# Where the convolution of a finished tile pair is issued inside the next Strassen unit

## The chip, the cores and the metric

The kernel runs on one core of a Trainium2 chip. The metric is device time in microseconds (us) of one execution, the median of several runs. TensorE multiplies, ScalarE runs activations and copies, VectorE (DVE in the rows) does the additions, GpSimd (POOL) issues the accumulating DMAs, and SyncE (SP) issues the plain loads.

## The reference, cut to what matters

One decoder layer on 512 tokens of width 2048. The part that the change touches is the first half of the gated MLP: an up-projection, a causal convolution of width 3 along the tokens, and a product of the two halves.

```python
def conv_ffn(h, w_up, conv_w, conv_b, w_down):
    u = h @ w_up                                   # (512, 2048) @ (2048, 2 * 5632)
    up = jnp.pad(u, ((0, 0), (CONV_WIDTH - 1, 0), (0, 0)))
    u = conv_b + sum(conv_w[i] * up[:, i:i + S] for i in range(CONV_WIDTH))
    a, b = jnp.split(u, 2, axis=-1)
    return (jax.nn.silu(a) * b) @ w_down
```

Everything is float32. A matmul operand is split into two parts, a rounded one and the rest, and products of parts are summed.

## The kernel before

**Units.** The up-projection makes 44 pairs of output tiles (128 channels by 512 tokens; tile `a` of the pair goes through the SiLU, tile `b` does not). Three pairs come from plain matmuls. The other 41 come from `unit`, one call for each pair (L228): a Winograd-Strassen product of 2x2 blocks, in which seven products named B11, T1, T2, B21, T3, B22 and T4 are issued in this order. Each is 8 matmuls of 512 columns with the rounded weights and 8 of 256 columns with the rest (T1: 16 of 256 and 8 of 256). A unit has three PSUM banks: r1 takes B11 and B21, r3 takes T1 and B22, and r2 takes T2, T3 and T4, each after the additions that read what was there before. For T3 these are L279 and L281, for T4 they are L294 and L296. Units alternate between the bank groups `acc` and `att`, so a unit's T4 and the next unit's B11 stand side by side in TensorE's queue.

**Weights.** A unit loads five 512 KB tiles, a11, a21, a22, a12 and d, into eight buffers named `raw` (L135, issued by SP). GpSimd adds a second block to d by an accumulating DMA (L242, `raw<-in_w_up`). L271 adds a22 to a21 (the sum s, for T1), L275 adds a11 to s (T2), and L299 adds s to a12 (B22). `parts` makes the two operands of each product: a rounded copy on ScalarE (L140, `wh`, three buffers) and the rest on VectorE (L142, `wl`, three buffers). Seven pairs of these are needed for a unit.

**Order.** The order of the instructions on each engine is fixed when the kernel is built, by a planner that takes what it reckons to be ready, earlier lines of the program first. Each engine then works through its own list. `issue_after` (in `behind`) adds that an instruction is queued behind a named one on its engine. In the profiled lists L271 of the next unit stands ahead of L275 of the unit at hand.

**The work between.** A unit calls `between(0)` after the copy of T1's bank, `between(1)` after the copies of B21's bank (L285, L287). In the up-projection the convolution of the pair before is issued at `between(1)`, all of it in a steady unit: `finish` with two `conv` (one activation L1032 and two additions of scaled shifts, L1033 and L1034, for each tile), the SiLU L1039, the product L1041 and the DMA of the result L1042.

Of the kernel before, what the change touches and what calls it, by code (L numbers as in the profile page):

```python
# [15 lines left out]
ALU = mybir.AluOpType  # L16
# [14 lines left out]
HALF = S // 2  # L31
# [44 lines left out]
def block_kernel(ctx: ExitStack, tc: tile.TileContext, A: dict, out: bass.AP):  # L76
# [11 lines left out]
    def t2k(tag, bufs, dt=F32, w=S):  # L88
        return sb.tile([P, w], dt, tag=tag, bufs=bufs, name=nm(tag))
# [7 lines left out]
    def slot(dt=F32, group=""):  # L97

        o = spare.pop((dt, group), None)
        if o is None:  # L100
            t = two(dt)
            o, spare[dt, group] = t[:, :S], t[:, S:]
        return o
# [12 lines left out]
    tt = nc.vector.tensor_tensor  # L116
# [16 lines left out]
    def load(src, w=1024):  # L133
        raw = t2k("raw", 8, w=w)
        nc.sync.dma_start(raw, src)  # L135
        return raw

    def parts(raw, w=1024):
        wh = t2k("wh", 3, F32R, w)
        act(wh, raw, AF.Copy)  # L140
        wl = t2k("wl", 3, F32R, w)
        tt(wl, raw, wh.bitcast(F32), ALU.subtract)  # L142
        return wh, wl
# [63 lines left out]
    def both(t):  # L207
        return t[:, :HALF], t[:, HALF:]
# [19 lines left out]
    def unit(src, f, between=lambda *_: None, wide=False, by_dma=False):  # L228

        n = len(f)
        w = n * P
        bank = (acc, att)[units[0] % 2]
        units[0] += 1
        r1, r2, r3 = (bank() for _ in range(3))

        def add(o, more):
            nc.gpsimd.dma_start(o, more, accum_op=ALU.add)  # L242

        def product(ps, a, name, first):
            ah, al = a
            for p in range(n):
                ops = [f[p][name]] if wide and name != "T1" else both(f[p][name])
                for i, b in enumerate(ops):
                    mm(ps[:, : b.shape[1]], ah[:, p * P : (p + 1) * P], b, start=first and p + i == 0, stop=False,  # L249
                       skip_group_check=True)  # L250
            for p in range(n):
                mm(ps[:, :HALF], al[:, p * P : (p + 1) * P], f[p][name][:, :HALF], start=False, stop=p == n - 1,  # L252
                   skip_group_check=True)

        a11 = load(src[0], w)
        a21 = load(src[2], w)
        a22 = load(src[3], w)
        a12 = load(src[1], w)
        if by_dma:
            d = load(src[2], w)  # L260
            add(d, src[0])
        product(r1, parts(a11, w), "B11", True)
        p = t2k("ta", 2)
        p1, p5 = both(p)
        if wide:
            act(p1, r1[:, HALF:], AF.Copy)
            last_v = tt(p1, r1[:, :HALF], p1, ALU.add)
        else:
            act(p1, r1[:, :HALF], AF.Copy)
        s = a21 if by_dma else t2k("raw", 8, w=w)  # L270
        last_v = tt(s, a21, a22, ALU.add)  # L271
        product(r3, parts(s, w), "T1", True)
        last = act(p5, r3[:, :HALF], AF.Copy, scale=-1.0)
        between(0, last, last_v)
        tt(s, s, a11, ALU.add)  # L275
        product(r2, parts(s, w), "T2", True)
        e = t2k("sp", 2)
        l1, u2 = both(e)
        last_v = tt(u2, p1, r2[:, :HALF], ALU.subtract)  # L279
        if wide:  # L280
            last_v = tt(u2, u2, r2[:, HALF:], ALU.subtract)  # L281
        product(r1, parts(a12, w), "B21", False)
        spare.pop((F32, "c"), None)
        c1, c2 = slot(group="c"), slot(group="c")
        last = act(c1[:, :HALF], r1[:, :HALF], AF.Copy)  # L285
        if wide:
            last = act(l1, r1[:, HALF:], AF.Copy)  # L287
        between(1, last, last_v)
        if by_dma:
            product(r2, parts(d, w), "T3", False)  # L290
        else:
            tt(a11, a11, a21, ALU.add)
            product(r2, parts(a11, w), "T3", False)
        tt(c2[:, HALF:], r2[:, :HALF], p1, ALU.subtract)  # L294
        if wide:
            tt(c2[:, HALF:], r2[:, HALF:], c2[:, HALF:], ALU.add)  # L296
        else:
            tt(c2[:, HALF:], c2[:, HALF:], p5, ALU.add)
        tt(a12, a12, s, ALU.add)  # L299
        product(r3, parts(a12, w), "B22", False)  # L300
        if wide:
            act(c1[:, HALF:], r3[:, :HALF], AF.Copy)
            tt(u2, r3[:, HALF:], u2, ALU.add)
            add(c1, e)
        else:
            tt(c1[:, HALF:], r3[:, :HALF], u2, ALU.add)
        product(r2, parts(a22, w), "T4", False)
        if wide:
            act(c2[:, :HALF], r2[:, :HALF], AF.Copy)
            tt(p1, r2[:, HALF:], p1, ALU.subtract)  # L310
            add(c2, p)
        else:
            tt(c2[:, :HALF], r2[:, :HALF], p1, ALU.subtract)
        return c1, c2
# [20 lines left out]
    @contextmanager  # L335
    def behind(*pins):

        with ExitStack() as stack:
            for p in pins:
                stack.enter_context(tc.issue_after(p.ins))  # L340
            yield
# [139 lines left out]
    for c in range(2):  # L481
        w = prep(A["w_qi7"][c])
        for k in range(8):
            i = 8 * c + k
# [153 lines left out]
    def some_ada(n=1, tag=("raw", 8)):  # L638
        for _ in range(n):
            if ada_left:  # L640
                ada_half(cb, *ada_left.pop(0), tag)
# [11 lines left out]
    for u in range(32):  # L653

        def between(i, *pins):
            with behind(*pins):
                next(work)
                if i:
                    some_ada()

        pair = unit(A["w_x"][u], f, between)
        for i, o in enumerate(pair):
            if u >= 16:
                sig = act(o, o, AF.Sigmoid)
            save(xd[2 * u + i], o)
# [138 lines left out]
    def stick_2(zs, soft):  # L804

        for n in (1, 2, 0):
            sp = of_soft(soft)[n]
            last = stt(sp, zs[n][:, : sp.shape[1]], 0.0, sp, ALU.max, ALU.add)
        one, two, three, _ = strips(*of_soft(soft))
        later = t2k("T", 2)  # L810
        a, b = later[:, 2 * P : 3 * P], later[:, : 2 * P]
        tt(a, two[:, P:], one, ALU.add)
        tt(b[:, :P], three[:, P : 2 * P], two[:, :P], ALU.add)
        tt(b[:, P:], three[:, 2 * P :], a, ALU.add)
        return (a, b), last
# [39 lines left out]
    for hd in range(NH):  # L855
# [12 lines left out]
        later, last = stick_2(*state)  # L868
# [32 lines left out]
    def sparse_2(p, s):  # L901
        nc.vector.reciprocal(s, s)
        for b in (2, 0, 1, 3):
            last = ts(p[b], p[b], s[:, b : b + 1], None, ALU.mult)
        return last
# [39 lines left out]
    for hd in range(NH):  # L945
        p, s, last = sparse_1(*pairs[hd])
# [7 lines left out]
        last = sparse_2(p, s)  # L954
# [14 lines left out]
    for j in range(KT):  # L969
# [9 lines left out]
        last = tt(g, g, t, ALU.add)  # L979
# [18 lines left out]

    def between(i, *pins):
        with behind(*pins):  # L1000
            if i:
                some_ada()

    sums = []
    for u in range(KT // 2):
        xr = []
        for j in (2 * u, 2 * u + 1):
            xr.append(t2k("w", 2))
            nc.gpsimd.dma_start(xr[-1], A["x"][j])
        for i, c in enumerate(unit(A["w_o"][u], f, between)):  # L1010
            j = 2 * u + i
            stt(c, c, mod[:, 32 + j : 33 + j], xr[i], ALU.mult, ALU.add)
            nc.gpsimd.dma_start(x1d[j], c)
            squares(c, j, sums)
# [15 lines left out]
    def conv(u, j):  # L1030
        t = t2k(("w", "T")[j % 2], 2)
        act(t, u, AF.Identity, scale=cw[:, j, 2:3], bias=cw[:, j, 3:4])  # L1032
        stt(t[:, 1:], u[:, : S - 1], cw[:, j, 1:2], t[:, 1:], ALU.mult, ALU.add)  # L1033
        stt(t[:, 2:], u[:, : S - 2], cw[:, j, 0:1], t[:, 2:], ALU.mult, ALU.add)  # L1034
        return t

    def finish(j, ua, ub):
        a = conv(ua, 2 * j)
        act(a, a, AF.Silu)  # L1039
        b = conv(ub, 2 * j + 1)  # L1040
        tt(a, a, b, ALU.mult)  # L1041
        nc.gpsimd.dma_start(yd[j // 2][:, j % 2 * S : (j % 2 + 1) * S], a)  # L1042


    ups = [bank() for bank in (acc, att) for _ in range(NU)]
# [27 lines left out]
    ups = [evac(ps) for ps in ups]  # L1073
    ready = [(j, *ups[2 * j : 2 * j + 2]) for j in range(NU)]

    def between(i, *pins):
        if len(ready) > 1 - i:
            with behind(*pins):
                finish(*ready.pop(0))

    finish(*ready.pop(0))
    for j in range(NU, NJ):
# [60 lines left out]
    def add_first(j, o):  # L1143
        t = t2k("w", 2)
        save(t, sumd[j])
        tt(o, o, t, ALU.add)
        save(sumd2[j], o)

    def between(i, *pins):
        if ready:  # L1150
            with behind(*pins):
                add_first(*ready.pop(0))

# [35 lines left out]
    j = KT - 1  # L1189
    ps = acc(), acc()  # L1190
    prepare(j)
    last = t2k("w", 2)
# [111 lines left out]
```

## Time and profile before

| what | value |
|---|---|
| median of 3 runs | 2863.05 us (2857.27 to 2873.1) |
| the profiled execution, its own time | 2858.4 us |
| its span on the core | 2856.6 us |
| granted clock of TensorE, mean of the span | 0.995 |
| the stage of the 41 units (first L296 to last L296) | 828.7 us for 40 units |

The span runs from the first to the last instruction of the program; the time of the execution holds it and 1.8 us around it. Busy times are sums over the records of an engine. An engine's idle time is put down to what released the next instruction.

### The profile page before, as it was taken

Reading aid. Unit: us, or ns where it says so; the run is one execution under the profiler, and the core shown is the slowest. Engines: PE = TensorE matmul, PEld = TensorE weight load, DVE = VectorE, ACT = ScalarE, POOL = GpSimd, SP = SyncE. Lnnn points to the kernel's source line nnn. Section 1 sums busy time; section 2 is a strip of 40 time slices with the busy share of each in tenths; the row PEclk is TensorE's granted clock in tenths of the full one; section 3 lists DMA queues with packets and bytes.
Section 4 is the critical chain, followed back from the end, with each engine's and each line's share of the span. In section 5 each row is a group of like instructions: output and inputs, shape, how many; then the busy total and the mean of one; then the engine's idle time right before and its main releaser. Section 6 shows DMA issues by size and latency. Waiting matters only on the chain.

```text
span 2856.6 us, 44877 instructions
## 1 busy us (share of the span) xinstructions
PE 2772.5 (97%) x17174; PEld 2464.7 (86%) x17174; DVE 2370.6 (83%) x3489; ACT 1410.4 (49%) x2083; POOL 391.6 (14%) x588
## 2 busy tenths in 40 slices
PE   7999999999999999999989999999999999999998
PEld 6779999999998768889988888888888888887887
DVE  8979888888897898899988888788888887887555
ACT  5544444455546655444465545455555555444221
POOL 0000000001011202111301111111111111111111
PEclk9999999999999999999999999999999999999999
DMA  9964456655565548665446767777677777668654
GB/s 348 347 228 143 166 179 211 201 177 171 180 225 191 180 152 303 242 197 203 155 159 165 200 178 193 184 190 196 182 199 184 200 192 239 176 196 292 230 185 137
DMA packets 176167, 576.88 MB, mean 202 GB/s; under 512 B 22144, under 2 KB 26624, under 8 KB 175952
## 3 DMA queue, kind: packets, MB, share of 16 engines
q1 hardware_dynamic: 123312, 421.06, 43.5%
q0 software_dynamic: 52192, 152.57, 20.3%
q8 instruction: 135, 2.21, 0.3%
q14 instruction: 80, 0.66, 0.1%
q10 hardware_dynamic: 448, 0.39, 0.0%
HBM read 487.78 MB, written 60.46 MB: 192 GB/s over the span
## 4 chain that ended last, share of the span: by engine, by line
PE 58%; DVE 16%; DMA 12%; issue 8%; ACT 5%; POOL 0%; DVEq 0%; SPq 0%; ACTq 0%; POOLq 0%
PE acc L249 12%; PE att L249 12%; DMA raw<-in_w_up 9%; DVE wl L142 6%; PE acc L252 6%; PE att L252 6%; ACT wh L140 3%; PE acc L152 3%; PE acc L153 3%; PE acc L154 3%; PE att L154 3%; PE att L152 3%; PE att L153 3%; DVE raw L333 2%; DVE raw L275 2%
## 5 line engine op out<-in xcount | busy, mean ns | idle before, releaser
L140 ACT ACTIVATE wh<-raw 128x1024 fp32r<-128x1024 f32 (+2 forms) x787 | 809.7, 1041 | 945.0 <-DVE raw L275 197.9
L142 DVE TENSOR_TENSOR wl<-raw,wh 128x1024 fp32r<-128x1024 f32 (+2 forms) x787 | 940.4, 1209 | 149.9 <-ACT wh L140 148.7
L249 PE MATMUL acc<-F,wh 128*128 128x256 f32 (+1 forms) x3840 | 653.6, 318 | 11.8 <-DVE F L296 7.1
L249 PE MATMUL att<-F,wh 128*128 128x256 f32 (+1 forms) x3776 | 640.2, 318 | 16.0 <-DVE F L296 9.0
L249 PEld LDWEIGHTS acc<-F,wh 128*128 128x128 f32 x3840 | 544.4, 191 | 60.9 <-DVE F L296 12.5
L249 PEld LDWEIGHTS att<-F,wh 128*128 128x128 f32 x3776 | 533.4, 191 | 65.8 <-DVE F L296 14.7
L252 PE MATMUL acc<-F,wl 128*128 128x256 f32 x2520 | 352.3, 283 | 0.0
L252 PE MATMUL att<-F,wl 128*128 128x256 f32 x2464 | 344.5, 282 | 0.0
L252 PEld LDWEIGHTS acc<-F,wl 128*128 128x128 f32 x2520 | 333.8, 191 | 11.9
L252 PEld LDWEIGHTS att<-F,wl 128*128 128x128 f32 x2464 | 326.3, 191 | 11.4
L333 DVE SCALAR_TENSOR_TENSOR raw<-raw,raw 128x1024 f32<-128x1024 f32 x186 | 226.9, 1230 | 70.4 <-DMA raw<-in_w_ada 70.4
L152 PE MATMUL acc<-F,wh 128*128 128x512 f32 (+2 forms) x476 | 179.0, 385 | 15.7 <-ACT F L173 15.7
L153 PE MATMUL acc<-F,wh 128*128 128x512 f32 (+2 forms) x476 | 182.2, 383 | 0.0
L154 PE MATMUL acc<-F,wl 128*128 128x512 f32 (+2 forms) x476 | 181.8, 382 | 0.0
L271 DVE TENSOR_TENSOR raw<-raw,raw 128x1024 f32<-128x1024 f32 x89 | 108.8, 1222 | 79.8 <-DMA raw<-in_w_up 70.8
L154 PE MATMUL att<-F,wl 128*128 128x512 f32 x394 | 155.5, 395 | 6.1 <-DVE wl L142 6.1
L152 PE MATMUL att<-F,wh 128*128 128x512 f32 x394 | 154.0, 397 | 2.7 <-ACT wh L140 2.7
L153 PE MATMUL att<-F,wh 128*128 128x512 f32 x394 | 154.8, 393 | 0.3 <-DVE F L174 0.2
L152 PEld LDWEIGHTS acc<-F,wh 128*128 128x128 f32 (+1 forms) x476 | 88.9, 188 | 35.4 <-ACT F L173 17.5
L275 DVE TENSOR_TENSOR raw<-raw,raw 128x1024 f32<-128x1024 f32 x89 | 109.5, 1230 | 1.0
L299 DVE TENSOR_TENSOR raw<-raw,raw 128x1024 f32<-128x1024 f32 x89 | 108.8, 1222 | 1.4
L153 PEld LDWEIGHTS acc<-F,wh 128*128 128x128 f32 (+1 forms) x476 | 89.4, 188 | 19.2 <-DVE F L174 1.8
(307 smaller groups left out, 3427.0 us busy)
## 6 DMA issues: line engine op xcount, KB each, us to landing
raw<-in_w_up SPq DMA_DIRECT2D x205, 512.0 KB, 4.4
raw<-in_w_ada SPq DMA_DIRECT2D x186, 512.0 KB, 5.0
raw<-in_w_x SPq DMA_DIRECT2D x128, 512.0 KB, 4.0
raw<-in_w_down SPq DMA_DIRECT2D x64, 512.0 KB, 4.5
raw<-in_w_up POOLq DMA_DIRECT2D x41, 512.0 KB, 8.8
xd<-F POOLq DMA_DIRECT2D x64, 256.0 KB, 2.6
F<-xd POOLq DMA_DIRECT2D x64, 256.0 KB, 5.0
raw<-in_w_o SPq DMA_DIRECT2D x32, 512.0 KB, 3.9
```

Source lines behind the costliest of these rows:

```text
L140: act(wh, raw, AF.Copy)
L142: tt(wl, raw, wh.bitcast(F32), ALU.subtract)
L152: mm(ps, ah, bh, start=first, stop=False, skip_group_check=not check)
L153: mm(ps, ah, bl, start=False, stop=False, skip_group_check=not check)
L154: mm(ps, al, bh, start=False, stop=last, skip_group_check=not check)
L249: mm(ps[:, : b.shape[1]], ah[:, p * P : (p + 1) * P], b, start=first and p + i == 0, stop=False, skip_group_check=True)
L252: mm(ps[:, :HALF], al[:, p * P : (p + 1) * P], f[p][name][:, :HALF], start=False, stop=p == n - 1, skip_group_check=True)
L271: last_v = tt(s, a21, a22, ALU.add)
L275: tt(s, s, a11, ALU.add)
L299: tt(a12, a12, s, ALU.add)
L333: stt(raw, raw, 1.0, cb[half], ALU.mult, ALU.mult, accum_out=macc[:, t, half : half + 1])
```

## The change

`finish` is cut into three steps, and `unit` calls `between` in a third place, after L296 and the addition that reads r2 last before T4. In a steady unit of the up-projection the convolution of tile `a` with its SiLU is now issued at `between(0)`, the convolution of tile `b` at `between(1)`, and the product of the two with the DMA of the result at `between(2)`, pinned behind the addition of L296 on VectorE. The other stages ignore the third place. The first of the 41 units, which has two pairs to finish, does one whole at `between(0)` and the second in steps.

```diff
@@ unit
         if wide:
-            tt(c2[:, HALF:], r2[:, HALF:], c2[:, HALF:], ALU.add)
+            last_v = tt(c2[:, HALF:], r2[:, HALF:], c2[:, HALF:], ALU.add)
         else:
-            tt(c2[:, HALF:], c2[:, HALF:], p5, ALU.add)
+            last_v = tt(c2[:, HALF:], c2[:, HALF:], p5, ALU.add)
+        between(2, last, last_v)
         tt(a12, a12, s, ALU.add)
@@
-    def finish(j, ua, ub):
+    def finish_steps(j, ua, ub):
         a = conv(ua, 2 * j)
         act(a, a, AF.Silu)
+        yield
         b = conv(ub, 2 * j + 1)
+        yield
         tt(a, a, b, ALU.mult)
         nc.gpsimd.dma_start(yd[j // 2][:, j % 2 * S : (j % 2 + 1) * S], a)
+        yield
+
+    def finish(*args):
+        for _ in finish_steps(*args):
+            pass
@@
+    steps = []
+
     def between(i, *pins):
-        if len(ready) > 1 - i:
-            with behind(*pins):
+
+        with behind(*pins):
+            if i == 0 and len(ready) > 1:
                 finish(*ready.pop(0))
+                return
+            if not steps:
+                steps.append(finish_steps(*ready.pop(0)))
+                if i == 1:
+                    next(steps[0])
+            next(steps[0])
+            if i == 2:
+                steps.pop()
```

The input-projection's `between` returns at once for i == 2, the one of the output projection acts for i == 1 alone, and the one of the down-projection for i < 2.

## Rows read from the trace of the kernel before

**Rows 1.** The page, part 1: busy us of each engine.

```profile
PE 2772.5 (97%) x17174; PEld 2464.7 (86%) x17174; DVE 2370.6 (83%) x3489; ACT 1410.4 (49%) x2083; POOL 391.6 (14%) x588
```

**Rows 2.** Busy time by windows: 40 units, then one late unit.

```profile
1535.32:2364.02 828.70, 806.39 (x4808) 707.73 (x4807) 693.26 (x883) 429.18 (x645) 126.80 (x159) 1.00 0.72 192
...
2283.78:2303.43 19.65, 19.65 (x123) 17.62 (x122) 17.50 (x23) 10.88 (x17) 3.21 (x4) 1.00 0.74 200
```

**Rows 3.** Waits of TensorE in the 40 units: us, times, longest.

```profile
PE att L249 <- DVE F L296: 9.0, 18, 0.6
PE acc L249 <- DVE F L296: 7.1, 15, 0.6
PE att L249 <- ACT wh L140: 3.0, 7, 1.1
PE acc L249 <- ACT wh L140: 2.4, 6, 0.6
```

**Rows 4.** Waits of VectorE in the same 40 units, all of them.

```profile
DVE raw L271 <- DMA raw<-in_w_up: 70.8, 38, 3.3
DVE wl L142 <- ACT wh L140: 61.6, 80, 1.1
DVE sp L279 <- PE acc L252: 1.4, 1, 1.4
```

**Rows 5.** VectorE's timeline over one unit: start, length, idle before.

```profile
1916.01 1.23 DVE L271 TENSOR_TENSOR raw<-raw,raw 128x1024 f32<-128x1024 f32 x1 [2.49 <-DMA raw<-in_w_up]
...
1921.30 2.35 DVE L142 TENSOR_TENSOR wl<-raw,wh 128x1024 fp32r<-128x1024 f32 x2
1923.57 1.22 DVE L299 TENSOR_TENSOR raw<-raw,raw 128x1024 f32<-128x1024 f32 x1
...
1925.15 0.42 DVE L281 TENSOR_TENSOR sp<-sp,att 128x256 f32<-128x256 f32 x1
1925.99 2.36 DVE L142 TENSOR_TENSOR wl<-raw,wh 128x1024 fp32r<-128x1024 f32 x2 [0.42 <-ACT wh L140]
1928.27 0.75 DVE L1033 SCALAR_TENSOR_TENSOR w<-F,cw,w 128x511 f32<-128x511 f32 x1
...
1930.91 0.42 DVE L294 TENSOR_TENSOR F<-att,ta 128x256 f32<-128x256 f32 x1
1931.25 0.69 DVE L1041 TENSOR_TENSOR w<-w,T 128x512 f32<-128x512 f32 x1
1931.85 0.42 DVE L296 TENSOR_TENSOR F<-att,F 128x256 f32<-128x256 f32 x1
...
1936.32 1.23 DVE L271 TENSOR_TENSOR raw<-raw,raw 128x1024 f32<-128x1024 f32 x1 [1.45 <-DMA raw<-in_w_up]
```

**Rows 6.** SP's timeline: issue of the last load before L271, three units.

```profile
1928.38 0.33 SPq L135 DMA_DIRECT2D raw<-in_w_up  x1
...
2260.63 0.33 SPq L135 DMA_DIRECT2D raw<-in_w_up  x1
...
2280.16 0.33 SPq L135 DMA_DIRECT2D raw<-in_w_up  x1
```

**Rows 7.** DMA issues at 1928: KB, us to landing (accumulating, then plain).

```profile
raw<-in_w_up POOLq DMA_DIRECT2D x1, 512.0 KB, 8.6
raw<-in_w_up SPq DMA_DIRECT2D x1, 512.0 KB, 7.8
```

**Rows 8.** TensorE's timeline in that unit: T3's start, then T4's.

```profile
1925.72 2.08 PE L249 MATMUL att<-F,wh 128*128 128x512 f32 x8
...
1932.32 2.11 PE L249 MATMUL att<-F,wh 128*128 128x512 f32 x8 [0.55 <-DVE F L296]
```

**Rows 9.** ScalarE's timeline in that unit.

```profile
1921.86 0.37 ACT L273 ACTIVATE ta<-att 128x256 f32<-128x256 f32 x1
1924.90 2.01 ACT L140 ACTIVATE wh<-raw 128x1024 fp32r<-128x1024 f32 x2 [2.67 <-DVE raw L299]
...
1927.34 0.81 ACT L1032 ACTIVATE w<-F,cw 128x512 f32<-128x512 f32 x1
```

**Rows 10.** DMA issue at 2280.16: KB, us to landing.

```profile
raw<-in_w_up SPq DMA_DIRECT2D x1, 512.0 KB, 7.0
```

**Rows 11.** VectorE's timeline: L271 of three units near the stage's end.

```profile
2248.25 1.23 DVE L271 TENSOR_TENSOR raw<-raw,raw 128x1024 f32<-128x1024 f32 x1 [1.66 <-DMA raw<-in_w_up]
...
2267.03 1.22 DVE L271 TENSOR_TENSOR raw<-raw,raw 128x1024 f32<-128x1024 f32 x1
...
2287.29 1.23 DVE L271 TENSOR_TENSOR raw<-raw,raw 128x1024 f32<-128x1024 f32 x1 [0.50 <-DMA raw<-in_w_up]
```

More of the change, by code (lines that the diff above doesn't have):

```diff
@@ L1000, in between @@
         with behind(*pins):
-            if i:
+            if i == 1:
                 some_ada()
@@ L1074, in block_kernel @@
     ready = [(j, *ups[2 * j : 2 * j + 2]) for j in range(NU)]
+    steps = []
     def between(i, *pins):
-        if len(ready) > 1 - i:
-            with behind(*pins):
+        with behind(*pins):
+            if i == 0 and len(ready) > 1:
                 finish(*ready.pop(0))
+                return
+            if not steps:
+                steps.append(finish_steps(*ready.pop(0)))
+                if i == 1:
+                    next(steps[0])
+            next(steps[0])
+            if i == 2:
+                steps.pop()
     finish(*ready.pop(0))
@@ L1149, in between @@
     def between(i, *pins):
-        if ready:
+        if ready and i < 2:
             with behind(*pins):
```

## The prediction

> **What bounds the kernel now.** I read the page first. TensorE is busy 97% of the span [rows 1], which says little about a stage in which it is held back a little in every unit. So I went to the 41 units of the up-projection, the only stage whose order of work changes, and read five views of it.
>
> The windows give the price of a unit: 828.7 us for 40 units, 20.72 us each, at a granted clock of 1.00. A late unit without any gap on TensorE takes 19.65 us [rows 2]. So 1.07 us are lost in a unit, 43 us in 40 units, and nothing that shortens waits can win more than these.
>
> The waits of TensorE name two places. 16.1 us stand before T4, which waits for L296 to have read bank r2 (33 units), and 5.4 us before a product whose rounded weights are late (13 units) [rows 3]. The wait before T4 is what the third place of the change deals with: in the unit shown L294 comes right behind the four additions of the convolution, then the product L1041 takes 0.6 us, then L296 runs, and T4 starts 0.05 us after L296 ends, having idled 0.55 us [rows 5, 8].
>
> But the gap on TensorE is where the loss is seen and not yet what sets the period. The waits of VectorE list what its queue stops for: the DMA before L271 (70.8 us, 38 of 40 units), ScalarE's rounded copies, and TensorE only once, for 1.4 us [rows 4]. VectorE's list therefore runs without regard to TensorE, and what comes round in it is a loop with the DMA. L271 starts when a22 of the next unit has landed; behind it in the list stand L275, the rests for T2, B21 and T3, then L299, L279, L281 and the rests for B22 and T4. The end of T4's rest frees a `raw` buffer, and SP issues the next a22 into it. In the unit shown L271 starts at 1916.01, the issue is at 1928.38, which is 12.37 us later, the load takes 7.8 us, and L271 of the next unit starts at 1936.32 [rows 5 to 7]. 12.4 + 7.8 + 0.1 = 20.3 us is that unit's period to the tenth. The first part is the same in a late unit, 2248.25 to 2260.63 or 12.38 us [rows 6, 11]; units differ by their load. With the mean of 20.72 us it is some 8.2 us. TensorE, which needs only 19.65 us, must idle somewhere for the rest, and it does so at whichever addition is late next: T4's bank, or T2's weights.
>
> The Trainium skill (Perfetto Trace Analysis, section Identifying the Most-Contended Engine and the strategy behind it) says that a gap that repeats can mean too few buffers for the next tile. The trace agrees: the wait of L271 repeats in 38 of 40 units, and the load behind it waits for a `raw` buffer.
>
> **The change, part by part.**
>
> *The convolution of tile a, moved to between(0).* Its activation is queued behind L273, which runs at 1921.86 to 1922.23 on ScalarE; then the activation (0.81) ends about 1923.0 [rows 9]. VectorE ends T3's rest at 1923.57 and turns to L299 [rows 5]. So the two additions of tile a are ready about when L299 starts, and being earlier in the program than L279 and the rests for B22 and T4 they go before these, around L299. Four such additions take 1928.27 to 1930.91, 0.66 us each [rows 5], two 1.32 us. VectorE now idles 0.42 us before B22's rest, for L299's result to pass ScalarE; the two additions cover that. T4's rest, and with it the load of a22, comes 1.32 - 0.42 = 0.9 us later. That is the low end. The high end is that L299 itself goes behind both: then the wait for ScalarE (1.0 for one copy [rows 9]) isn't covered, and the delay is nearer 2.0 us. I take 0.9, since the planner put L299 right behind T3's rest. The move can't be free: in each order both additions stand before T4's rest.
>
> *What that does to the load.* Here rows give two bounds. If the load lands as much later as it is issued, a unit takes 0.9 us more. If it lands when the accumulating DMA beside it lets it, nothing changes: that DMA is issued once T3's rest has freed d's buffer and d has landed, ahead of the moved additions. It takes 8.6 us beside the load's 7.8 [rows 7], so both end together. One unit tests this: there the issue came 13.13 us after L271 (2267.03 to 2280.16) instead of 12.4, and the load took 7.0 us [rows 6, 10, 11]. The next L271 followed after 20.26 us, no later than in the mean unit. This is nearer to the second bound, and I take +0.2 us a unit. Most of the delay is hidden by the accumulating DMA; without that cover it costs the whole 0.9.
>
> The Trainium skill (DMA: Bandwidth & Descriptors, section Issuing engines are not separate DMA queues) says that transfers of all queues share 16 engines and interleave. By that alone a load that starts later loses its head start on the accumulating one and the whole delay would show, 36 us in 40 units. The one unit that tests it says less; the DMA engines are busy 0.72 of the stage [rows 2].
>
> *T3's bank.* L281 ends at 1925.57, and T3 starts at 1925.72 [rows 5, 8]: no room is left. With 0.66 to 1.32 us in front of it T3 will wait that long where it now hardly waits. This wait replaces the one before T4: with T3 1.2 us later, T4 can't start before L296 has gone anyway. VectorE has nothing new to wait for in this.
>
> *The convolution of tile b, left at between(1).* The same two additions and activation, at the same place, behind L281. Nothing.
>
> *The product, moved behind L296.* L296 runs 0.6 us sooner, and since the convolution's second half alone stands before L294, T4's bank is free about 1.0 us sooner than now. The 16.1 us before T4 go. L1041 now stands before B11's rest of the next unit; 0.6 us there are covered by the idle time before L271, 1.45 to 2.49 us in the rows [rows 5]. The DMA of the result moves with it on GpSimd's queue, by a few tenths, ahead of the same accumulating DMAs as before.
>
> *Sum.* Removing the wait before T4 gives nothing as long as the loop lasts 20.7 us: TensorE idles the same 1.07 us elsewhere. The loop grows by 0.2 us: 40 x 0.2 = 8 us. Against the profiled execution's 2858.4 us that is 2866 us; the median of the runs before lies 4.7 us above that execution.
>
> **The rivals.**
>
> *Slower: the delay reaches the landing.* The place is the load of a22, the price 0.9 us a unit, 36 us in all, 2894 us; with L299 behind both additions up to 2.0 us, 80 us, 2938 us. It decides from the point where the load, having lost its head start, ends after the accumulating DMA. For it: the DMA engines are busy 0.72 of the time, and the load issued at 2260.63, whose L271 started 6.4 us later without any wait [rows 6, 11], shows what timing against the other DMA can be worth. Against: the unit at 2280.16.
>
> *Faster: the gap on TensorE is what it seems.* If the planner's new order puts L271 of the next unit behind L275, the queue is no longer stopped by the DMA ahead of T2's weights. The loop is cut by the time from L271 to the rest for T2, more than the 1.07 us lost, and TensorE runs at 19.65 us: 43 us less, 2815 us. Removing the 16.1 us before T4 alone gives 2842 us. For it: L271's place depends on what the planner reckons, and later loads push it back. Against: none of the edits moves L271 itself.
>
> *The change doesn't do what it says,* because the planner issues the pieces where they were: unlikely, the pin behind L296 forces the product, and tile a's operands have long landed. It would give 2858 us, in the forecast's range.
>
> **How the numbers follow.** The forecast (2850 to 2878) has 0.45, the slower rival 0.33 (0.07 of it beyond 2905), the faster 0.22 (about half below 2822). The range 2822 to 2905 leaves out somewhat under 2 in 10. Faster or slower by 0.5% (14 us, about what a measurement of this kernel can tell from no change): the forecast gives 0.36 to no change, 0.07 to slower, 0.02 to faster. With the rivals, faster 0.24, same 0.37, slower 0.39.
>
> **What would show it.** In the profile after: the wait of T4 for L296 gone; a wait of T3 for L281 of about 1 us a unit in its place; two additions L1033 and L1034 before the rests for B22 and T4; the issue of a22 some 13.3 us after L271 and the load nearer 7.5 us than 8.2; L271 still waiting for the DMA in nearly every unit; a period near 20.9 us. The forecast is wrong if L271 stands elsewhere in VectorE's list, if the load takes 8.2 us or more from its later issue, or if TensorE's waits fall in sum.

## The result and the profile after

The changed kernel took 2908.18 us (2905.06 to 2912.05, 4 runs) beside 2866.99 us of the kernel before: a ratio of 1.015, 95% interval 1.011 to 1.018. It is slower by 41 us. The forecast of no change was wrong, and the time lies 3 us above the range. Of the kernel called before_pin below one of four executions took 8100 us, for a reason that the record doesn't show, and its time is the median of the other three.

The profiled execution took 2910.49 us, its span is 2908.7 us. The windows of the changed kernel, first to last L296 of the 41 units, answer to the first of [rows 2] (length, then busy us of TensorE, its weight loads, VectorE, ScalarE, GpSimd; granted clock; DMA share; GB/s):

```profile
1538.50:2410.80 872.30, 811.46 (x4803) 719.81 (x4804) 703.53 (x884) 438.11 (x646) 126.53 (x159) 0.98 0.68 182
```

40 units take 872.3 us, 21.81 each, against 20.72. The difference of 1.09 us a unit, 43.6 us in all, is the loss. Outside this stage the two profiled executions differ by another 8.5 us, 3.1 ahead of it and 5.4 behind it, which was not followed up; with them the two spans differ by 52 us, where the medians differ by 41. VectorE is busy for 10 us more and TensorE for 5, in a stage that is 43 us longer: this is waiting, not work.

Waits of TensorE in the changed kernel over these units (us, times, longest), as in [rows 3]:

```profile
PE acc L249 <- DVE sp L281: 31.5, 16, 2.5
PE att L249 <- DVE sp L281: 25.9, 17, 2.5
PE acc L249 <- ACT wh L140: 1.9, 3, 1.5
PE att L249 <- ACT wh L140: 1.2, 1, 1.2
```

The waits for L296 are gone, as the change means to, and T3 waits for L281 instead, 57.4 us in 33 units. Read by itself this view says that a gap has moved one product forward and grown. The waits of VectorE, against [rows 4]:

```profile
DVE raw L271 <- DMA raw<-in_w_up: 93.7, 39, 3.7
DVE wl L142 <- ACT wh L140: 37.4, 48, 1.3
DVE F L294 <- PE acc L252: 19.2, 17, 2.1
DVE F L294 <- PE att L252: 13.0, 17, 2.0
```

VectorE still stops for the DMA ahead of L271 in 39 of 40 units, and for longer. It now waits for TensorE too, at L294, but that stands behind T4's rest, where there is time to spare before the next L271. VectorE's timeline over one unit of the changed kernel, to be laid beside [rows 5]:

```profile
1936.19 1.22 DVE L271 TENSOR_TENSOR raw<-raw,raw 128x1024 f32<-128x1024 f32 x1 [2.63 <-DMA raw<-in_w_up]
1937.34 0.42 DVE L304 TENSOR_TENSOR sp<-acc,sp 128x256 f32<-128x256 f32 x1
1937.67 1.22 DVE L142 TENSOR_TENSOR wl<-raw,wh 128x1024 fp32r<-128x1024 f32 x1
1938.92 1.23 DVE L275 TENSOR_TENSOR raw<-raw,raw 128x1024 f32<-128x1024 f32 x1
1940.06 0.42 DVE L311 TENSOR_TENSOR ta<-acc,ta 128x256 f32<-128x256 f32 x1
1941.33 2.36 DVE L142 TENSOR_TENSOR wl<-raw,wh 128x1024 fp32r<-128x1024 f32 x2 [0.85 <-ACT wh L140]
...
1943.94 1.22 DVE L300 TENSOR_TENSOR raw<-raw,raw 128x1024 f32<-128x1024 f32 x1
1945.08 1.22 DVE L142 TENSOR_TENSOR wl<-raw,wh 128x1024 fp32r<-128x1024 f32 x1
1946.21 0.74 DVE L1036 SCALAR_TENSOR_TENSOR w<-F,cw,w 128x511 f32<-128x511 f32 x1
1946.99 0.75 DVE L1037 SCALAR_TENSOR_TENSOR w<-F,cw,w 128x510 f32<-128x510 f32 x1
...
1949.12 0.41 DVE L281 TENSOR_TENSOR sp<-sp,att 128x256 f32<-128x256 f32 x1
1949.45 1.22 DVE L142 TENSOR_TENSOR wl<-raw,wh 128x1024 fp32r<-128x1024 f32 x1
...
1957.63 1.23 DVE L271 TENSOR_TENSOR raw<-raw,raw 128x1024 f32<-128x1024 f32 x1 [2.38 <-DMA raw<-in_w_up]
```

What differs between L271 and T4's rest is this. Tile a's two additions (L1036, L1037) stand behind T3's rest (the L142 at 1945.08), as expected. And L304 (before: L303) with T1's rest (the L142 at 1937.67) stand behind L271, which no line of the diff asks for: the order fixed at build came out otherwise. Smaller moves came with it: L311 (before: L310) went behind L275, into the time in which VectorE waits for ScalarE, and L300 (before: L299) went ahead of T3's rest. In the kernel before L310 is the one that stands between L271 and L275, and L303 and T1's rest come ahead of L271, as its own timeline shows:

```profile
1917.15 0.42 DVE L310 TENSOR_TENSOR ta<-acc,ta 128x256 f32<-128x256 f32 x1
1917.48 1.22 DVE L275 TENSOR_TENSOR raw<-raw,raw 128x1024 f32<-128x1024 f32 x1
...
1933.31 0.43 DVE L303 TENSOR_TENSOR sp<-att,sp 128x256 f32<-128x256 f32 x1
1933.64 1.22 DVE L142 TENSOR_TENSOR wl<-raw,wh 128x1024 fp32r<-128x1024 f32 x1
```

There L303 and T1's rest filled time in which VectorE waits for the DMA anyway. Behind L271, L304 only takes the place that L310 had; what is added is T1's rest, and L275 starts 2.73 us after L271 instead of 1.47. All that stands behind, up to the loads, is pushed back. SP's timeline has the issue of d (1945.22) and of a22 (1950.70) in that unit of the changed kernel:

```profile
1945.22 0.33 SPq L135 DMA_DIRECT2D raw<-in_w_up  x1
...
1950.70 0.33 SPq L135 DMA_DIRECT2D raw<-in_w_up  x1
```

d is asked for 9.03 us after L271 and a22 14.51 us after it. In the kernel before d was issued at 1923.68 in the unit of [rows 5]:

```profile
1923.68 0.33 SPq L135 DMA_DIRECT2D raw<-in_w_up  x1
```

which is 7.67 us after L271, and a22 12.37 (12.38 in the median of the units). So d comes 1.36 us later and a22 2.13. The a22 load then took less than the 7.8 us of [rows 7]; the changed kernel's DMA issues at 1950.70 (KB, us to landing):

```profile
raw<-in_w_up SPq DMA_DIRECT2D x1, 512.0 KB, 6.8
```

### The profile page after: what moved, and what is told of

Its sections match the earlier page's. It is cut to its first block, busy times and chain, and to the rows that moved or that the text cites. A ratio compares the mean times of both kernels' runs of the same rounds, so it can differ in the third digit from the quotient of the medians.

```text
span 2908.7 us, 44994 instructions
## 1 busy us (share of the span) xinstructions
PE 2785.7 (96%) x17174; PEld 2484.4 (85%) x17174; DVE 2379.9 (82%) x3489; ACT 1418.2 (49%) x2083; POOL 390.6 (13%) x588
## 4 chain that ended last, share of the span: by engine, by line
PE 56%; DVE 21%; DMA 12%; issue 6%; ACT 4%; POOL 0%; DVEq 0%; SPq 0%; ACTq 0%; POOLq 0%
PE att L249 11%; PE acc L249 11%; DMA raw<-in_w_up 8%; DVE wl L142 7%; PE att L252 5%; PE acc L252 5%; PE acc L152 3%; PE acc L153 3%; PE acc L154 3%; PE att L154 3%; PE att L152 3%; PE att L153 3%; ACT wh L140 2%; DVE raw L334 2%; DVE raw L275 2%
## 5 line engine op out<-in xcount | busy, mean ns | idle before, releaser
L142 DVE TENSOR_TENSOR wl<-raw,wh 128x1024 fp32r<-128x1024 f32 (+2 forms) x787 | 942.9, 1208 | 131.2 <-ACT wh L140 129.9
L249 PEld LDWEIGHTS acc<-F,wh 128*128 128x128 f32 x3840 | 550.5, 192 | 82.7 <-ACT wh L140 34.6
L271 DVE TENSOR_TENSOR raw<-raw,raw 128x1024 f32<-128x1024 f32 x89 | 108.8, 1222 | 103.3 <-DMA raw<-in_w_up 93.7
L275 DVE TENSOR_TENSOR raw<-raw,raw 128x1024 f32<-128x1024 f32 x89 | 109.8, 1233 | 2.2
L300 DVE TENSOR_TENSOR raw<-raw,raw 128x1024 f32<-128x1024 f32 x89 | 108.6, 1221 | 1.4
```

## The experiments

"Loop" stands for L271, VectorE's list, the loads, L271 of the next unit. All ratios are to the kernel before, run on the same chip. The table collects the loop's parts from VectorE's and SP's timelines: the two issues are medians after L271, the load's length a mean, each over the units of the stage; the period is the stage from first to last L296 divided by 40, in the profiled execution.

| kernel | d asked, us | a22 issued, us | a22's load, us | period, us | time, us | ratio (95%) |
|---|---|---|---|---|---|---|
| before | 7.67 | 12.38 | 8.2 | 20.72 | 2860.6 to 2867.0, by chip | |
| changed | 9.03 | 14.51 | 7.2 | 21.81 | 2908.2 | 1.015 (1.011 to 1.018) |
| product_alone | 7.34 | 12.05 | 7.9 | 20.20 | 2844.5 | 0.995 (0.993 to 0.996) |
| tile_a_alone | 9.03 | 14.51 | 7.3 | 21.88 | 2914.7 | 1.020 (1.018 to 1.022) |
| t1_late | 8.60 | 13.30 | 8.2 | 21.45 | 2889.9 | 1.010 (1.007 to 1.014) |
| after_t1 | 7.40 | 15.36 | 5.8 | 21.35 | 2887.0 | 1.008 (1.006 to 1.009) |
| dose1 | 7.34 | 12.67 | 7.7 | 20.63 | 2854.7 | 0.997 (0.996 to 0.998) |

In each row the issue of a22, its load and 0.1 us make the period, to 0.2 us. Where L271 starts as soon as a22 has landed this sum has to come out; it shows that the loop closes in these kernels, and what shows that the loop holds the time are the edits below.

**The two halves of the change.** First the product alone, with both convolutions at `between(1)`:

```diff
+            if i == 0:
+                if len(ready) > 1:
+                    finish(*ready.pop(0))
+                return
             if not steps:
                 steps.append(finish_steps(*ready.pop(0)))
-                if i == 1:
-                    next(steps[0])
+                next(steps[0])
             next(steps[0])
```

> Both convolutions stay at between(1); only the product and its DMA are issued behind L296. Theory A (the period is a loop: L271, VectorE's list as far as T4's rest, the load of the next a22, L271 again): the list as far as T4's rest holds the same work, so the issue of the load stays 12.0 to 12.4 us after L271 and a unit stays at 20.4 to 20.8 us; the time is 0 to 13 us below the kernel before, although the wait of T4 for L296 goes. Theory B (TensorE's gaps set the period): the 16 us of waits before T4 and the refill behind them are won, 16 to 33 us.

It is 16 us faster, a little beyond theory A's bound and at the edge of B's. The profile decides between them: TensorE's waits for L296 fell only from 16.1 to 10.5 us, and the loop got shorter by as much as the period, because L310 fell behind L275, 0.33 us, and the load took 0.3 us less. L296 did not come sooner by the move: B11's rest (1.2 us) took the place between L294 and L296 where the product (0.7 us) had stood. Waits of TensorE in this kernel:

```profile
PE att L249 <- DVE F L296: 5.8, 10, 0.6
PE acc L249 <- DVE F L296: 4.7, 9, 0.6
```

Then tile a alone, with tile b and the product at `between(1)`:

```diff
+            if i == 2:
+                return
             if not steps:
@@
-            if i == 2:
+            if i == 1:
+                next(steps[0])
                 steps.pop()
```

> Tile a at between(0), tile b and the product at between(1). Theory A: as in the changed kernel two additions and T1's rest stand between L271 and T4's rest, the issue comes 14.5 us after L271, a unit takes 21.6 to 21.9 us and the time is 36 to 45 us above the kernel before. Theory B: the same wait of T3 for L281 (1.7 us a unit), and beside it the wait of T4 for L296 again, so 50 to 70 us above the kernel before.

All of the loss is here, and some more: 54 us, above theory A's 36 to 45 too; less the 16 us that the product won it is 38, near the 41 of the whole change. T4's waits for L296 did not come back, so theory B's sum does not hold, though its total would fit; the loop's parts are those of the changed kernel.

**L271 out of the way.** One edit, made in either kernel: L271 of the next unit is queued behind L275.

```diff
+        if by_dma and at_t2:
+            with behind(at_t2.pop()):
+                last_v = tt(s, a21, a22, ALU.add)
...
-        tt(s, s, a11, ALU.add)
+        v = tt(s, s, a11, ALU.add)
+        at_t2[:] = [v]
```

> The kernel before with one edit: L271 of the next unit is queued behind L275 of the unit at hand, so that VectorE no longer stops for the DMA ahead of T2's sum. Theory A: the list from L271 to the issue of the load shrinks to some 9.3 us, 9.3 + 8 is below TensorE's own 19.65 us, and a unit takes 19.65 to 19.9 us: 30 to 43 us below the kernel before. Theory B: the wait of T4 for L296 has not been touched, only the 5 us of waits for T2's weights go: at most 10 us below.

> The changed kernel with the same edit to L271. Theory A: the list from L271 to the issue shrinks to some 11 us, with the load of 7.2 us 18.2 us, below 19.65: a unit takes 19.65 to 20.0 us and the time falls 25 to 43 us below the kernel before, some 70 to 80 us below the changed kernel. Theory B: the two additions of tile a still stand ahead of L281, T3 still waits 1.7 us a unit, and the time stays 30 us or more above the kernel before.

2820.6 us (ratio 0.986, 0.984 to 0.989) and 2824.6 us (0.988, 0.986 to 0.990). The edit takes 40 us from the kernel before; from the changed one it takes some 77 us, the 41 us that it stood above the kernel before and the 36 us that it now stands below it. The two end within 4 us. The pin also changed the rest of VectorE's list, so what it shows is that with L271 out of the way tile a's place costs nothing that stands clear of the noise. The windows and VectorE's waits of before_pin over 40 units:

```profile
1539.70:2327.90 788.20, 788.14 (x4808) 705.54 (x4807) 697.74 (x883) 440.79 (x645) 126.80 (x159) 1.00 0.74 202
```

```profile
DVE wl L142 <- ACT wh L140: 43.8, 41, 1.1
DVE sp L285 <- PE acc L253: 21.5, 20, 1.4
DVE sp L285 <- PE att L253: 20.4, 19, 1.1
DVE raw L274 <- DMA raw<-in_w_up: 1.2, 2, 1.0
```

TensorE has no gap in 788 us, 19.70 us a unit, and now VectorE waits for it, at L285 (L279 before), in 39 units. The wait for the DMA is down to 1.2 us.

The product alone with the same pin:

> The product alone behind L296, and L271 queued behind L275. Theory A: TensorE sets the period at 19.65 us; 37 to 43 us below the kernel before, within 5 us of the pin without the product's move, since T4's wait is worth nothing where no list is late.

2825.6 us (0.986, 0.985 to 0.988): no more than the pin by itself. With the pin TensorE has no gap left that the product's move could close. What T4's bank is worth when it is freed sooner this run doesn't show, since here too B11's rest stands between L294 and L296 in the product's place.

An idle addition behind L296 made the planner put L271 behind L275 by itself:

```diff
+        if by_dma:
+            with behind(v):
+                tt(junk[0], junk[0], junk[0], ALU.add)
```

> The kernel before with an idle addition of 128x1024 (1.13 us) a unit on VectorE behind L296. With it the order fixed at build puts L271 of the next unit behind L275, as the pin did. Theory A: more work for VectorE, but no list between the DMA and T2's sum: a unit takes 19.65 to 20.2 us and the time falls 20 to 43 us below the kernel before. Theory B: VectorE has 1.13 us a unit more to do, the wait of T4 for L296 remains: no gain, up to 20 us above.

2822.0 us (0.985, 0.983 to 0.987): 1.13 us more work on VectorE in each unit, and 41 us less.

**The DMA side.** Both kernels without the accumulating DMA, so that the T3 product is another one:

```diff
-            add(d, src[0])
```

> The kernel before without the accumulating DMA of L242 into d: the tile d is left as loaded. Theory A: the load of a22 no longer shares the DMA engines with it and takes 4 to 5 us; 12.4 + 4.5 = 16.9 is below TensorE's 19.65, so a unit takes 19.65 to 19.9 us and the time falls 30 to 43 us below the kernel before. Theory B: T4 still waits for L296 and the time stays within 10 us.

> The changed kernel without that accumulating DMA. Theory A: 14.5 + 4.5 = 19.0 is just below 19.65, so a unit takes 19.65 to 20.0 us, and the time comes within 12 us of the kernel before without the DMA. Theory B: the additions of tile a still hold back T3's bank, and the time stays 40 us or more above that kernel.

2821.0 us (0.985, 0.983 to 0.987) and 2825.8 us (0.987, 0.985 to 0.989). The a22 load takes 4.2 and 4.1 us, TensorE sets the period (19.69 and 19.68 us), and T3's wait for L281 is gone although nothing ahead of L281 has moved.

Then the same DMA kept, but issued after T4's rest, with no change in VectorE's list:

```diff
+                with behind(after_t4.pop()):
+                    add(d, src[0])
...
+            after_t4[:] = [nc.gpsimd.tensor_copy(tiny, a[1][:, :1].bitcast(F32))]
```

> The kernel before with one edit on GpSimd's queue: a copy of one column of T4's rest ahead of the accumulating DMA into d, so that this DMA is issued after T4's rest, together with the load of a22 and not 0.6 us ahead of it. VectorE's and ScalarE's lists are the same as before. Theory A2: a22 gets ahead of the accumulating DMA and lands in 5 to 6 us (as in the one unit at 2260, 5.2 us); 12.4 + 5.5 = 17.9 is below 19.65, so TensorE sets the period: 30 to 43 us below the kernel before. Theory A1 without the sharing: no change, since issue and list are the same. Theory B: no change.

> The changed kernel with the same edit; VectorE's list is that of the changed kernel. Theory A2: 14.5 + 5.5 = 20.0 us a unit at most, 60 to 90 us below the changed kernel, 0 to 43 us below the kernel before, and T3's wait for L281 shrinks though nothing ahead of L281 has moved. Theory B: T3 waits as in the changed kernel, 40 to 50 us above the kernel before.

2820.3 us (0.984, 0.983 to 0.986), the fastest of all, and 2843.7 us (0.992, 0.991 to 0.994). GpSimd's timeline of late_add shows the DMA issued at 1951.49; a22 had gone at 1950.76:

```profile
1950.87 0.68 POOL L315 COPY tiny<-wl 128x1 f32<-128x1 f32 x1 [10.50 <-DVE wl L142]
1951.49 0.87 POOL L244 DMA_DIRECT2D raw<-in_w_up  x1
```

and a22's load, by that kernel's DMA issues, took

```profile
raw<-in_w_up SPq DMA_DIRECT2D x1, 512.0 KB, 5.4
```

0.7 us ahead of the accumulating DMA instead of 0.65 us behind it, and the load is some 3 us shorter (5.2 us in the mean, against 8.2). In the changed kernel with this edit 14.7 + 5.2 + 0.1 = 20.0 us is still above 19.65, and T3 still waits for L281 a little:

```profile
PE att L251 <- DVE sp L287: 5.8, 11, 1.0
...
PE acc L251 <- DVE sp L287: 2.2, 4, 0.8
```

8.0 us in place of 57.4, with the same two additions ahead of L281. So that wait follows from the loop; it isn't what sets the period.

**Which part of the list.** A delay of T4's rest alone, by one idle addition behind L281:

> The kernel before with one idle addition of 128x1024 (1.13 us) a unit on VectorE, behind L281 and ahead of B22's rest; nothing else moves in VectorE's list. T3's bank is free as early as before, and L294 and L296 come 0.7 us later. Theory A (the loop sets the period): 0.42 us of the addition are covered by the wait for B22's rounded copy, so the issue of the load stands 13.1 us after L271 instead of 12.4; by the changed kernel, where half of the delay reached the landing, a unit takes 0.3 to 0.7 us more and the time is 12 to 28 us above the kernel before. Theory B (TensorE's wait for bank r2 sets the period): T4's wait grows by the 0.7 us of the delay, 28 us above. Theory C (only the wait of T3 for L281 costs): no change. A and B are told apart by the rows, A by issue plus load making the period to 0.1 us.

2854.7 us: 8 us faster, where both theories had it slower. The addition delayed a22 by 0.29 us, less than the 0.7 expected, and d came 0.33 us sooner, because something else did move in VectorE's list: L267, which stood behind T2's rest, went ahead of it into the wait for ScalarE. The period, 0.09 us shorter, went with d; the profiled execution, 2861 us, was the slowest of twelve. That made a second version of theory A: the loop closes through d as well, since the accumulating DMA follows d's landing and a22 lands with it.

T1's rest put ahead of L271 again in the changed kernel:

```diff
+        if by_dma and at_t1:
+            with behind(at_t1.pop()):
+                last_v = tt(s, a21, a22, ALU.add)
...
+        at_t1[:] = [tt(wl, s, wh.bitcast(F32), ALU.subtract)]
```

> The changed kernel with L271 of the next unit queued behind T1's rest of the unit at hand. In VectorE's list T1's rest and L304 no longer stand between L271 and T3's rest, so d is asked for some 7.4 us after L271 instead of 9.0; but tile a's additions and now tile b's stand ahead of T4's rest, so the load of a22 is issued some 14.9 us after L271, as late as in the changed kernel or later. Theory A1 (the loop closes through the load of a22): 14.9 + 7.2 = 22.1 us a unit, 40 to 60 us above the kernel before. Theory A2 (the loop closes through T3's rest, the load of d, 3.5 us, and the accumulating DMA into it, beside which a22 can't land before 8.6 to 9.0 us): 7.4 + 3.5 + 0.6 + 8.8 + 0.1 = 20.4 us a unit, 5 to 20 us below the kernel before. Theory B (T3's wait for L281): L281 is still behind tile a's additions, 25 us or more above the kernel before.

2887.0 us, 20 us above the kernel before, between A1 and A2 and outside both. d came as early as A2 says (7.40 us), but tile b's additions too went ahead of T4's rest, with a wait for ScalarE, and a22 was issued 15.36 us after L271. The load took 5.8 us, less than in any other kernel that issues it behind that DMA. So a22 doesn't simply land with the accumulating DMA: issued 3.9 us behind it instead of 0.65, a load is 2.4 us shorter, which gives back most of the delay and not all. T3 did not wait for L281 as theory B has it; TensorE idled at T2's weights, where VectorE is late by the DMA:

```profile
PE att L250 <- ACT wh L140: 30.1, 19, 3.0
PE acc L250 <- ACT wh L140: 19.3, 18, 2.3
PE att L250 <- DVE sp L290: 0.2, 1, 0.2
```

Last, the kernel before with T1's rest alone moved behind L310 (the convolution stays):

```diff
+        if by_dma and at_end:
+            with behind(at_end.pop()):
+                tt(wl, s, wh.bitcast(F32), ALU.subtract)
```

> The kernel before with one instruction moved in VectorE's list: T1's rest is queued behind L310, and so behind L271 of the next unit, as in the changed kernel's list; the convolution stays whole at between(1), behind T4's rest. Theory A2 (what counts is what stands between L271 and the load of d, since the accumulating DMA and with it a22 follow from there): d is asked for 1.15 us later after L271, 8.8 us, a22 13.5 us after it, the distance between the two DMAs stays, so the whole 1.15 us shows: a unit takes 21.7 to 22.0 us, 40 to 50 us above the kernel before, as much as the whole change costs. Theory E (tile a's convolution ahead of T4's rest and of L281 is what costs, with a22 or with T3's bank): no convolution has moved, so at most 10 us above.

2889.9 us, 29 us slower (ratio 1.010, 1.007 to 1.014), short of A2's 40 to 50 and far above E's 10. Its VectorE timeline:

```profile
1971.09 1.23 DVE L272 TENSOR_TENSOR raw<-raw,raw 128x1024 f32<-128x1024 f32 x1 [1.63 <-DMA raw<-in_w_up]
1972.23 0.42 DVE L319 TENSOR_TENSOR ta<-acc,ta 128x256 f32<-128x256 f32 x1
1972.56 1.22 DVE L278 TENSOR_TENSOR wl<-raw,wh 128x1024 fp32r<-128x1024 f32 x1
1973.81 1.23 DVE L284 TENSOR_TENSOR raw<-raw,raw 128x1024 f32<-128x1024 f32 x1
1974.95 0.42 DVE L268 TENSOR_TENSOR ta<-att,ta 128x256 f32<-128x256 f32 x1
```

T1's rest (L278) stands behind L271 (L272 here), and d and a22 are both asked for 0.92 us later. L275 (L284) starts 1.25 us later; 0.33 us of this come back because L267 (L268) went ahead of T2's rest here too. The distance between the two DMAs stays, and of the 0.92 us 0.73 show in the period. TensorE's granted clock is 1.00 in these 40 units, so this loss owes nothing to the clock.

## Why the prediction was wrong, point by point

**What bounds the kernel: right.** The period is the loop of L271, VectorE's list and a22's load. It held in every kernel in which L271 waits (the table, and after_late_add), and each of three ways to open it (the pin, no accumulating DMA, the later accumulating DMA) brought the period to TensorE's 19.7 us, from the kernel before each time.

**The waits that come and go: right in kind.** T4's wait is gone, T3's came in its place, 1.7 us in each of 33 units where 0.66 to 1.32 was expected. That taking T4's wait away wins nothing while the loop lasts agrees with the changed kernel and with tile a alone, where the wait is gone and the time rose; no run takes away that wait and nothing else. Two smaller points were wrong and cost nothing. VectorE does have something new to wait for, TensorE at L294, 32 us in 34 units. And the product's move doesn't by itself bring L296 forward, since B11's rest takes the product's place.

**The step that failed** is "What that does to the load": the +0.2 us a unit, which measured +1.09. It rested on the sentence that the accumulating DMA is issued "ahead of the moved additions", so that only a22 is late and most of its delay is hidden beside that DMA. As to the additions this held: they stand behind what frees the buffer for d, and they bring a22 0.77 us further behind d, where 0.9 was expected. What failed is the other half, that d and the accumulating DMA are not late. The new order put T1's rest behind L271, which the prediction didn't consider: it took the rest of VectorE's list as it was, save L271 itself. So d, the accumulating DMA and a22 all came 1.36 us later, with little to hide it. (The load of d even follows another instruction now: SP issues it at 1945.22, as L300 ends at 1945.16, and not with T3's rest, which ends at 1946.30.) T1's rest moved in the kernel before costs 0.73 us a unit (t1_late), 29 of the 41 us, with d 0.92 us later. At that rate the 1.36 us of the changed kernel would cost 1.08 us: an estimate, 1.36 x 0.73 / 0.92, which is nearly all of the 1.09. The further 0.77 us of a22 go with a load that is 1.0 us shorter. That part of the forecast, most of the delay hidden beside the accumulating DMA, agrees with this and with after_t1, where 3 us more of a22's delay cost 0.6 us. The 14.51 us from L271 to a22 stood outside the prediction's 13.3 for the same reason.

**The rivals.** The slower one had the sign and nearly the size (36 us), but by another way: it had a22 alone late and the delay reaching the landing. The head start that it has the load lose was never there: a22 is issued 0.65 us behind the accumulating DMA in the kernel before. The faster one named its mechanism rightly: L271 behind L275 gave 2821 and 2822 us where it said 2815; only the change doesn't do that.

**Left open.** Why the order fixed at build put T1's rest behind L271, and why L267 and L310 move with other edits, was not looked into. Whether tile a's additions cost nothing with T1's rest left ahead of L271 was not shown in one clean run, since after_t1 moved tile b as well. In 40 units of the changed kernel the granted clock averaged 0.98 instead of 1.00; TensorE waits there and is busy 5 us longer, and this was not tested by itself.

## What to carry to other kernels

A gap on the busiest engine shows who was late, not what sets the period: follow the engine it waited for until the chain comes back to itself, and add up the loop; if list plus load makes the period, try an edit that shortens this loop and nothing else. An in-order engine that waits for a DMA early in its list delays all that stands behind, so put what doesn't need the DMA ahead of it, and look at what a rebuilt order does to instructions that the diff never touches. Here one addition queued behind another (2821 us) was worth 40 us, or one DMA issued 0.7 us behind a load instead of 0.65 us ahead of it (2820 us) 46 us, while the change meant for the visible gap lost as much.

## What the runs showed of the hardware

A 512 KB load took 4.2 us where no accumulating DMA of the same size ran (before_noadd), 5.2 us when issued 0.7 us ahead of one (late_add), 8.2 us when issued 0.65 us behind it (before), 7.2 us at 1.45 us (changed), 6.5 us at 2.3 us (before_pin) and 5.8 us at 3.9 us (after_t1). Of these places the one just behind is the worst, and a step of 1.4 us in the order of the two was worth 3 us of load. That a load is shorter the later it stands behind that DMA the prediction had from one unit (7.0 us); the runs bear it out over these distances. What in the DMA engines makes it so, no run shows.
